# Squares and scaled norm tiles moved from SBUF to PSUM, and the first three projections after a norm run feature tile by feature tile

## The chip, the cores and the metric

The kernel runs on one core of a Trainium2 chip. The metric is the device time of one execution in microseconds. All arithmetic is float32; a product of two float32 matrices is made of three TensorE products of rounded parts (high times high, high times low, low times high).

Engines are named as the profile names them: PE is TensorE, PEld its weight loads, DVE is VectorE, ACT is ScalarE, POOL is GpSimd, SP is the engine that issues the DMAs. [...]

## The reference

Two layers of a transformer block with adaptive norms, on 512 tokens of width 1024, and a final norm. The four mixers are left out here, since the change does not touch them.

```python
def rmsnorm(x, g):
    y = xf * lax.rsqrt(jnp.mean(xf * xf, axis=-1, keepdims=True) + RMS_EPS)
    return (y * g).astype(x.dtype)

for l in range(DEPTH):                       # DEPTH = 2
    mod = c_act @ w_ada[l] + b_ada[l]
    sh1, sc1, g1, sh2, sc2, g2 = [t[:, None, :] for t in jnp.split(mod, N_ADA, axis=-1)]
    h = rmsnorm(x, norm_mix_g[l]) * (1.0 + sc1) + sh1
    z = h @ w_in[l]
    o = jnp.concatenate([swa_mixer(...), mla_mixer(...), nsa_mixer(...), moba_mixer(...)], axis=-1)
    x = x + g1 * (o @ w_out[l])
    h = rmsnorm(x, norm_mlp_g[l]) * (1.0 + sc2) + sh2
    x = x + g2 * (jnp.square(jax.nn.relu(h @ w_up[l])) @ w_down[l])
return rmsnorm(x, final_norm_g)
```

## The kernel before

The activations lie transposed: 8 feature tiles of 128 features (partitions) by 512 tokens (columns). The kernel is written with a scheduler that sets the order of each engine's queue when the program is built, from the program's own order, from what each instruction depends on and from an estimate of durations; the order is then fixed, and the scheduler adds the waits. Tiles come from pools with a fixed number of buffers for each tag; a new tile of a tag waits until the last reader of the tile that had its buffer is done.

PSUM has eight banks. Three belong to the tag `mm` (pool `psA`: the results of projections), two to `sc` (`psS`: attention scores and the broadcast of a norm), two to `pt` (`psT`: transposed attention weights), one to `po` (`psO`).

A product of a weight tile with the activations is `mm3` (lines 330 to 332): for each feature tile k three matmuls, high weight x high activation (L330), high weight x low activation (L331), low weight x high activation (L332). Weights come by DMA into a raw tile; ACT makes the high part (L89, `whi`), and POOL the low part by a subtraction of two tiles in SBUF (L91, `wlo`). There are four slots for high parts and four for low parts, and each is asked for three weight tiles ahead of its use. A slot falls free when the last matmul that reads it is done.

A norm and its neighbours run like this:

- `proj_x` (output projection, part 2, or down projection, part 5) makes the eight new tiles of the residual x. The first five are made over all 512 tokens. The last three (`HEAD = 3`) are made in two halves of 256 tokens: three groups for the first half, then `norm(0)`, then three groups for the second, then `norm(1)`. After each group DVE adds the result to x (L368), which also frees its PSUM bank.
- For each new tile of x, `Sums.add` squares it on ACT (L246, tile `sq`) and adds the square to a running sum on DVE (L247, `sqacc`); the very first square is written to the sum directly (L243).
- `norm_bcast` adds the sums over the partitions with four small matmuls (L277), raises to the power -1/2 on POOL (L257, after an L253 on DVE), and broadcasts the result to all partitions with matmuls (L263, tile `rsb`).
- `norm_tile` (L290 to L297) makes one feature tile of the normed activations for a half: DVE multiplies x by the gain column and `rsb` into a scaled tile t (L292, `ht`), ACT adds the shift and rounds to the high part (L294, `hhi`), DVE makes the low part from t, the shift and the high part (L295, `hlo`).
- `proj_head` (L336) makes the first three projections of the normed activations: all of the first half, group by group (for each group eight feature tiles), then all of the second half, group by group. Its three results take the three `mm` banks. Then the three evacuations follow, and `proj_T` makes the other projections one at a time, with 512 columns. In the MLP an evacuation is a relu on ACT (L1070), a square on DVE (L1071) and a split into high and low part (L398, L399). Before the mixers of layer 1 the first evacuation is a square and a scaled copy on ACT (L652, L653).

`tmp_tile` gives float32 tiles in SBUF, four buffers for all who use it, `sq` and `ht` among them. There are three places where norm and `proj_head` follow each other: in layer 0 before the MLP, in layer 1 before the mixers, and in layer 1 before the MLP. Layer 0 starts with `start` (L1085), which squares all of x, has a norm of its own (L1121 to L1131) while the weights of the adaptive part arrive and are reduced on DVE (L188), and runs the first five projections itself; of the lines changed it uses `Sums` alone. The final norm (`final_half`) uses `Sums` and writes its tiles out.

Of the kernel before, what the change touches and what calls it, by code (L numbers as in the profile page):

```python
# [10 lines left out]
F32 = mybir.dt.float32  # L11
F32R = mybir.dt.float32r
AF = mybir.ActivationFunctionType
ALU = mybir.AluOpType
# [3 lines left out]
P = 128  # L18
S = 512
D = 1024  # L20
KT = D // P
# [88 lines left out]
def layer_stack(ctx: ExitStack, tc: tile.TileContext, a, out):  # L110
    nc = tc.nc
# [8 lines left out]
    psT = ctx.enter_context(tc.tile_pool(name="psT", bufs=2, space=PSUM))  # L120
    psO = ctx.enter_context(tc.tile_pool(name="psO", bufs=1, space=PSUM))

    def mmbank(name):
        return psA.tile([P, 512], F32, tag="mm", name=name)

    def tmp_tile(name):
        return wkp.tile([P, S], F32, tag="tmp", name=name, bufs=4)
# [3 lines left out]
    X = {}  # L131
# [37 lines left out]
    for half in range(2):  # L169
        ps = psA.tile([P, 512], F32, tag="mm", name="cbp")  # L170
        for j in range(4):
            k = 4 * half + j
# [52 lines left out]
    H2 = S // 2  # L225

    def cols(half):
        return slice(0, S) if half is None else slice(half * H2, half * H2 + H2)

    class Sums:  # L230
# [6 lines left out]
        def add(self, k, half=None):  # L237
            for hv in (0, 1) if half is None else (half,):
                first = hv not in self.done
                self.done.add(hv)  # L240
            c = cols(half)
            if first:
                nc.scalar.activation(self.acc[:, c], X["x"][:, k, c], AF.Square)  # L243
            else:
                sq = tmp_tile("sq")
                nc.scalar.activation(sq[:, c], X["x"][:, k, c], AF.Square)  # L246
                nc.vector.tensor_tensor(self.acc[:, c], self.acc[:, c], sq[:, c], op=ALU.add)  # L247

# [39 lines left out]
        return gs  # L288

    def norm_tile(hh, k, c, rsb, gk, shk):  # L290
        t = tmp_tile("ht")
        nc.vector.scalar_tensor_tensor(t[:, c], X["x"][:, k, c], gk, rsb, op0=ALU.mult, op1=ALU.mult)  # L292
        hi, lo = hh[k]
        nc.scalar.activation(hi[:, c], t[:, c], AF.Identity, bias=shk)  # L294
        nc.vector.scalar_tensor_tensor(  # L295
            lo[:, c], t[:, c], shk, hi[:, c].bitcast(F32), op0=ALU.add, op1=ALU.subtract
        )  # L297

    def h_tiles(pool, tag, bufs):
# [5 lines left out]
    class Norm:  # L305
# [8 lines left out]
        def half(self, hv):  # L314
            rsb = norm_bcast(self.sums, hv)
            if self.hh is None:
                self.hh = self.mk()
                self.gcols = self.gs()
            for k in range(KT):
                norm_tile(  # L320
                    self.hh, k, cols(hv), rsb, self.gcols[:, k : k + 1],
                    mod[self.l][:, self.psh, k : k + 1],
                )


    def mm3(ps, w, h, k, first, last, c=slice(0, S)):

        wh, wl = w
        hh, hl = h
        nc.tensor.matmul(ps, wh[:, k, :], hh[:, c], start=first, stop=False)  # L330
        nc.tensor.matmul(ps, wh[:, k, :], hl[:, c], start=False, stop=False)  # L331
        nc.tensor.matmul(ps, wl[:, k, :], hh[:, c], start=False, stop=last)  # L332
# [3 lines left out]
    def proj_head(hs, evacs, step=None):  # L336

        evacs, rest = evacs[:HEAD], evacs[HEAD:]
        ws = [W.get() for _ in evacs]
        pss = [mmbank("pj") for _ in evacs]  # L340
        for half in range(2):
            c = cols(half)
            for g in range(len(evacs)):
                for k in range(KT):
                    mm3(pss[g][:, c], ws[g], hs[k], k, k == 0, k == KT - 1, c)
        for g, f in enumerate(evacs):
            f(pss[g])
            if step is not None:
                step()
        proj_T(hs, rest, step)  # L350

    def proj_T(hs, evacs, step=None):
        for f in evacs:
            w = W.get()
            ps = mmbank("pj")
            for k in range(KT):
                mm3(ps, w, hs[k], k, k == 0, k == KT - 1)
            f(ps)
            if step is not None:
                step()  # L360
# [41 lines left out]
    def attention_layer(l, n1, finish):  # L402
# [23 lines left out]
        with ExitStack() as es:  # L426
# [252 lines left out]
            if l == 0:  # L679
                for f, ps in zip(evacs[:3], pss):  # L680
                    f(ps)
            else:
                proj_head(hs, evacs[:3])
# [634 lines left out]
```

## Time and profile before

| | us |
|---|---|
| median of 3 runs | 1338.73 (1336.64 to 1339.17) |
| the profiled execution | 1340.61 |
| its span, first to last instruction | 1338.8 |
| PE busy in the span | 1257.1 (94%) |
| DVE, ACT, POOL busy | 765.2, 590.9, 512.1 |

A row of the timeline gives the start of an instruction (or of a run of equal ones, with x and their number), its duration, the engine, the line, what it writes and reads, and in brackets how long the engine had been idle before it and what ended that. The windows give for a stretch the busy time of PE with the number of its matmuls, the mean granted clock, and the traffic of the DMAs. Durations of matmuls overlap, so the distance between two starts is the better measure of their cost.

### The profile page before, as it was taken

The numbers are of one execution on the slowest core, as the hardware profiler recorded it, in microseconds if no ns is written. First come the engines' busy times: TensorE is split into PE (matmuls) and PEld (weight loads), VectorE is DVE, ScalarE is ACT, GpSimd is POOL, SyncE is SP. The second block draws the span as 40 slices with busy tenths as digits, with TensorE's granted clock in tenths as the row PEclk, the third lists the DMA queues.
The fourth block names the chain that finished last, engine by engine and source line by source line (L and its number), as shares of the span: only waits on it lengthen the run. The fifth ranks groups of instructions, "written<-read, shape, count | busy, mean of one in ns | idle before, by whom it ended". The sixth has DMA issues, their size and how long they took to land. (4 is left out here: it accounts for less than half of the span.)

```text
span 1338.8 us, 17560 instructions
## 1 busy us (share of the span) xinstructions
PE 1257.1 (94%) x6500; PEld 1049.3 (78%) x6500; DVE 765.2 (57%) x1609; ACT 590.9 (44%) x1145; POOL 512.1 (38%) x276
## 2 busy tenths in 40 slices
PE   3888999888999999999989899999999999999997
PEld 3676788768988888888889677878888888888886
DVE  6888878978445555454364887677753312213124
ACT  4346768683443132231234657687443313223220
POOL 4432232224344544545433432230534444444441
PEclk9989999999999999999989999999989999999999
DMA  8623233435246766766322221120423333333311
GB/s 334 209 98 127 64 111 111 140 126 206 69 131 185 244 212 209 239 190 204 130 93 90 94 95 64 51 74 11 166 80 94 94 95 95 96 97 98 102 49 64
DMA packets 49766, 168.69 MB, mean 126 GB/s; under 512 B 5648, under 2 KB 8336, under 8 KB 49680
## 3 DMA queue, kind: packets, MB, share of 16 engines
q1 hardware_dynamic: 49680, 167.57, 38.3%
q8 instruction: 51, 0.84, 0.2%
q14 instruction: 35, 0.29, 0.1%
HBM read 163.35 MB, written 4.19 MB: 125 GB/s over the span
## 5 line engine op out<-in xcount | busy, mean ns | idle before, releaser
L91 POOL TENSOR_TENSOR wlo<-raw,whi 128x1024 fp32r<-128x1024 f32 (+3 forms) x186 | 454.9, 2450 | 583.0 <-ACT whi L89 550.9
L89 ACT ACTIVATE whi<-raw 128x1024 fp32r<-128x1024 f32 (+3 forms) x186 | 193.7, 1045 | 437.7 <-PE px L331 237.5
L331 PE MATMUL pj<-hlo,whi 128*128 128x512 f32 (+1 forms) x783 | 297.3, 380 | 8.5 <-DVE hlo L295 8.4
L330 PE MATMUL pj<-hhi,whi 128*128 128x512 f32 (+1 forms) x783 | 296.0, 380 | 2.6 <-ACT hhi L1124 1.2
L332 PE MATMUL pj<-hhi,wlo 128*128 128x512 f32 (+1 forms) x783 | 294.7, 376 | 0.0
L330 PE MATMUL px<-a,whi 128*128 128x512 f32 (+1 forms) x560 | 208.4, 372 | 0.0
L332 PE MATMUL px<-a,wlo 128*128 128x512 f32 (+1 forms) x560 | 208.1, 372 | 0.0
L331 PE MATMUL px<-a,whi 128*128 128x512 f32 (+1 forms) x560 | 207.4, 370 | 0.0
L331 PEld LDWEIGHTS pj<-hlo,whi 128*128 128x128 f32 x783 | 150.8, 193 | 35.5 <-DVE hlo L295 11.4
L330 PEld LDWEIGHTS pj<-hhi,whi 128*128 128x128 f32 x783 | 150.4, 193 | 28.0 <-ACT hhi L1124 2.2
L332 PEld LDWEIGHTS pj<-hhi,wlo 128*128 128x128 f32 x783 | 150.7, 192 | 25.8
L368 DVE SCALAR_TENSOR_TENSOR x<-px,mod,x 128x512 f32<-128x512 f32 (+1 forms) x92 | 62.1, 678 | 171.1 <-PE px L332 162.1
L1071 DVE SCALAR_TENSOR_TENSOR t<-pj,r 128x512 f32<-128x512 f32 x64 | 44.3, 692 | 157.8 <-ACT r L1070 157.8
L188 DVE CUSTOM_DVE_ANT_0 adaw<-adaw,cb,vecs 128x1024 f32<-128x1024 f32 x78 | 105.2, 1349 | 43.8 <-DMA adaw<-in_wadaD 43.7
L332 PEld LDWEIGHTS px<-a,wlo 128*128 128x128 f32 x560 | 105.1, 188 | 19.2
L331 PEld LDWEIGHTS px<-a,whi 128*128 128x128 f32 x560 | 105.1, 188 | 18.8
L330 PEld LDWEIGHTS px<-a,whi 128*128 128x128 f32 x560 | 105.2, 188 | 17.9
L399 DVE TENSOR_TENSOR a<-t,a 128x512 fp32r<-128x512 f32 x64 | 71.8, 1122 | 44.7 <-ACT a L398 44.7
L540 ACT ACTIVATE e<-e,nm 128x256 f32<-128x256 f32 (+3 forms) x160 | 85.9, 539 | 14.6 <-DVE nm L535 14.4
L518 POOL TENSOR_SCALAR e<-e,rc 128x128 f32<-128x128 f32 x40 | 24.3, 608 | 143.2 <-DVE rc L545 67.1
L399 DVE TENSOR_TENSOR pl<-pt,ph 128x512 fp32r<-128x512 f32 (+1 forms) x112 | 65.3, 597 | 4.4 <-ACT ph L398 3.3
L574 PE MATMUL pt<-ident,e 128*128 128x128 f32 x376 | 61.7, 278 | 3.6 <-DVE pl L399 1.5
(236 smaller groups left out, 1932.7 us busy)
## 6 DMA issues: line engine op xcount, KB each, us to landing
adaw<-in_wadaD SPq DMA_DIRECT2D x78, 512.0 KB, 4.4
raw<-in_wup SPq DMA_DIRECT2D x64, 512.0 KB, 3.5
raw<-in_wdown SPq DMA_DIRECT2D x64, 512.0 KB, 3.5
raw<-in_winT SPq DMA_DIRECT2D x28, 512.0 KB, 3.6
ada<-in_wadaP SPq DMA_DIRECT2D x16, 512.0 KB, 7.2
raw<-in_wout SPq DMA_DIRECT2D x16, 512.0 KB, 3.5
x<-in_xT SPq DMA_DIRECT2D x8, 512.0 KB, 5.1
cw<-in_cw SPq DMA_DIRECT2D x8, 512.0 KB, 4.9
```

The lines of the kernel that those rows point to most:

```text
L89: self.nc.scalar.activation(vh[0:rows], raw[0:rows], AF.Copy)
L91: eng.tensor_tensor(vl[0:rows], raw[0:rows], vh[0:rows].bitcast(F32), op=ALU.subtract)
L188: nc.vector.tensor_tensor_reduce(out=w, in0=w, in1=cb, scale=1.0, scalar=vecs[:, off : off + 1], op0=ALU.mult, op1=ALU.add, accum_out=mod[ ...
L330: nc.tensor.matmul(ps, wh[:, k, :], hh[:, c], start=first, stop=False)
L331: nc.tensor.matmul(ps, wh[:, k, :], hl[:, c], start=False, stop=False)
L332: nc.tensor.matmul(ps, wl[:, k, :], hh[:, c], start=False, stop=last)
L368: last["dve"] = nc.vector.scalar_tensor_tensor(X["x"][:, m, c], ps, mod[l][:, part, m : m + 1], X["x"][:, m, c], op0=ALU.mult, op1=ALU.add)
L399: last["dve"] = nc.vector.tensor_tensor(lo, src, hi.bitcast(F32), op=ALU.subtract)
L518: nc.gpsimd.tensor_scalar_mul(e, e, r)
L540: nc.scalar.activation(e, e, AF.Exp, bias=nm[:, n : n + 1], scale=-1.0, accum_out=den[:, n : n + 1])
L574: nc.tensor.transpose(pt[:, c : c + P], p[n][:, col : col + P], ident)
L1071: nc.vector.scalar_tensor_tensor(t, ps, 0.0, r, op0=ALU.max, op1=ALU.mult)
```

## The change

Three edits. The square of `Sums.add` and the scaled tile of `norm_tile` are taken from the tag `pt` in PSUM (two buffers, shared with each other and with the transposes of attention) instead of from the four SBUF buffers of `tmp_tile`; the scaled tile takes a whole bank and uses 256 of its columns. And in `proj_head` the loops over feature tiles and over the three groups change places: in each half, the three matmuls of group 0, 1 and 2 for feature tile 0, then for feature tile 1, and so on.

```diff
@@ Sums.add
-                sq = tmp_tile("sq")
+                sq = psT.tile([P, S], F32, tag="pt", name="sq")
                 nc.scalar.activation(sq[:, c], X["x"][:, k, c], AF.Square)
                 nc.vector.tensor_tensor(self.acc[:, c], self.acc[:, c], sq[:, c], op=ALU.add)
@@ norm_tile
-        t = tmp_tile("ht")
-        nc.vector.scalar_tensor_tensor(t[:, c], X["x"][:, k, c], gk, rsb, op0=ALU.mult, op1=ALU.mult)
+        t = psT.tile([P, 512], F32, tag="pt", name="ht")[:, 0:H2]
+        nc.vector.scalar_tensor_tensor(t, X["x"][:, k, c], gk, rsb, op0=ALU.mult, op1=ALU.mult)
         hi, lo = hh[k]
-        nc.scalar.activation(hi[:, c], t[:, c], AF.Identity, bias=shk)
+        nc.scalar.activation(hi[:, c], t, AF.Identity, bias=shk)
         nc.vector.scalar_tensor_tensor(
-            lo[:, c], t[:, c], shk, hi[:, c].bitcast(F32), op0=ALU.add, op1=ALU.subtract
+            lo[:, c], t, shk, hi[:, c].bitcast(F32), op0=ALU.add, op1=ALU.subtract
         )
@@ proj_head
-            for g in range(len(evacs)):
-                for k in range(KT):
+            for k in range(KT):
+                for g in range(len(evacs)):
                     mm3(pss[g][:, c], ws[g], hs[k], k, k == 0, k == KT - 1, c)
```

## Rows read from the trace of the kernel before

**Rows 1.** The page, part 1: busy us (share of the span), number of instructions.

```profile
PE 1257.1 (94%) x6500; PEld 1049.3 (78%) x6500; DVE 765.2 (57%) x1609; ACT 590.9 (44%) x1145; POOL 512.1 (38%) x276
```

**Rows 2.** Four lines of DVE: ns shortest/median/longest, first and last start, shapes.

```profile
L295 DVE SCALAR_TENSOR_TENSOR hlo<-ht,mod,hhi x48: 468/478/2500, 321.4 to 983.8; 128x256 fp32r<-128x256 f32 x48
L247 DVE TENSOR_TENSOR sqacc<-sqacc,sq x47: 409/679/2927, 6.7 to 1329.5; 128x256 f32<-128x256 f32 x24, 128x512 f32<-128x512 f32 x23
L368 DVE SCALAR_TENSOR_TENSOR x<-px,mod,x x92: 469/750/752, 297.1 to 1328.4; 128x512 f32<-128x512 f32 x68, 128x256 f32<-128x256 f32 x24
L399 DVE TENSOR_TENSOR pl<-pt,ph x112: 403/678/693, 111.0 to 930.7; 128x512 fp32r<-128x512 f32 x72, 128x256 fp32r<-128x256 f32 x32, 128x384 fp32r<-128x384 f32 x8
```

**Rows 3.** Groups by line, DVE, 682 to 697 us: busy us, mean ns, idle before.

```profile
L295 DVE SCALAR_TENSOR_TENSOR hlo<-ht,mod,hhi 128x256 fp32r<-128x256 f32 x8 | 9.3, 1166 | 0.3 <-ACT hhi L294 0.3
```

**Rows 4.** Timeline of DVE and of POOL, layer 1 before the mixers.

```profile
684.72 2.34 DVE L295 SCALAR_TENSOR_TENSOR hlo<-ht,mod,hhi 128x256 fp32r<-128x256 f32 x1
...
684.37 2.41 POOL L91 TENSOR_TENSOR wlo<-raw,whi 128x1024 fp32r<-128x1024 f32 x1 [2.86 <-ACT whi L89]
687.03 2.41 POOL L91 TENSOR_TENSOR wlo<-raw,whi 128x1024 fp32r<-128x1024 f32 x1 [0.26 <-ACT whi L89]
```

**Rows 5.** Timeline of PE, same place.

```profile
695.85 0.58 PE L331 MATMUL pj<-hlo,whi 128*128 128x256 f32 x1 [1.93 <-DVE hlo L295]
```

**Rows 6.** Windows: length, PE busy (matmuls), granted clock, DMA share and GB/s.

```profile
327.00:351.80 24.80, 22.27 (x154) 0.86 0.16 52
688.60:696.00 7.40, 3.87 (x22) 0.95 0.53 185
696.00:702.00 6.00, 5.96 (x27) 0.50 0.30 90
702.00:715.00 13.00, 13.00 (x111) 1.00 0.34 110
...
965.80:991.40 25.60, 22.13 (x154) 0.87 0.20 62
```

**Rows 7.** Timeline of PE, layer 0, output projection and norm before the MLP.

```profile
297.95 0.47 PE L330 MATMUL px<-ohi,whi 128*128 128x512 f32 x1 [2.65 <-DVE x L368]
...
317.19 0.61 PE L277 MATMUL rsb<-ones,sqacc 128*128 128x1 f32 x4 [1.23 <-DVE sqacc L247]
...
318.85 0.71 PE L263 MATMUL rsb<-ident,rs 128*128 128x128 f32 x4 [0.48 <-POOL rs L257]
```

**Rows 8.** Timeline of DVE and ACT, second half of the norm at 700 us.

```profile
700.50 1.26 DVE L292 SCALAR_TENSOR_TENSOR ht<-x,gs,rsb 128x256 f32<-128x256 f32 x3 [2.09 <-PE rsb L263]
701.69 1.27 DVE L295 SCALAR_TENSOR_TENSOR hlo<-ht,mod,hhi 128x256 fp32r<-128x256 f32 x3
...
701.02 1.31 ACT L294 ACTIVATE hhi<-ht,mod 128x256 fp32r<-128x256 f32 x3 [6.52 <-DVE ht L292]
```

**Rows 9.** Windows of PE around 300 and 320 us, columns as in rows 6.

```profile
299.50:302.80 3.30, 3.30 (x9) 0.51 1.03 402
319.70:323.20 3.50, 3.50 (x19) 0.51 0.02 6
```

**Rows 10.** Timeline of ACT and DVE, evacuations in layer 1, MLP and mixers.

```profile
985.92 1.06 ACT L89 ACTIVATE whi<-raw 128x1024 fp32r<-128x1024 f32 x1 [2.18 <-issue]
987.01 0.60 ACT L1070 ACTIVATE r<-pj 128x512 f32<-128x512 f32 x1
...
988.90 1.04 ACT L89 ACTIVATE whi<-raw 128x1024 fp32r<-128x1024 f32 x1
...
987.64 0.69 DVE L1071 SCALAR_TENSOR_TENSOR t<-pj,r 128x512 f32<-128x512 f32 x1 [3.38 <-ACT r L1070]
...
710.49 0.68 ACT L653 ACTIVATE ckvg<-pj,vecs 128x512 f32<-128x512 f32 x1
```

**Rows 11.** Timeline of DVE and PE, start of layer 0.

```profile
9.88 5.03 DVE L247 TENSOR_TENSOR sqacc<-sqacc,sq 128x512 f32<-128x512 f32 x4
...
59.55 0.97 PE L330 MATMUL pj<-hhi,whi 128*128 128x512 f32 x3 [1.23 <-ACT hhi L1124]
```

## Prediction

> **What bounds the kernel now.** Read the page's busy times first. PE is busy 1257.1 of 1338.8 us [rows 1], so a change is worth what it takes out of PE's 82 us of idle time, or out of stretches where PE runs at a low clock. Nothing else reaches the end. The change touches the norms, so I looked at the three places where a half of a norm is followed by the first three projections: A (layer 0, before the MLP, 327 to 352 us), B (layer 1, before the mixers, 689 to 715) and C (layer 1, before the MLP, 966 to 991).
>
> Then the single lines, with their shortest, median and longest duration. L295, which makes the low part of a tile, takes 468 to 2500 ns in one shape, and L247 up to 2927; L368, of the same operation as L295 but with one input in PSUM, never takes over 752 in 92 (512 columns the most of them), nor L399 with its source in PSUM over 693 [rows 2]. L295 and L247 read two tiles in SBUF. In the first half at B eight L295 take 9.3 us [rows 3] where 8 x 0.478 would be 3.8, and the timeline shows what stretches three of them: one runs from 684.72 for 2.34 us, exactly while POOL runs an L91 (684.37 for 2.41 us) [rows 4]. A and C have the same pattern, three L295 of sixteen.
>
> [...]
>
> **Part 1: scaled tile and squares in PSUM.** L295 and L247 then have one input in PSUM and one in SBUF, as L368 and L399 have, so I price them at the shortest of those, 469 and 403 ns, and take all stretching away [rows 2]. Writing a tile to PSUM from DVE or ACT is not in the trace. The nearest rows are the same operations into SBUF and the PSUM reads of rows 2. I take no difference, with 60 ns either way per instruction: 22 tile and square operations a half, 1.3 us of DVE work beside PE work. [...]
>
> What is this worth? The floor of a place is 144 matmuls of 128x256 (2 halves x 3 groups x 8 tiles x 3). At full clock 111 take 13.0 us [rows 6], 0.117 each, so 16.9 us. With the four sums (0.61) and four broadcasts (0.71) of the second half [rows 7] it is 18.2 us. The stretches from the first matmul of the head to the end of its last are 24.8 us (A), 26.4 (B: 7.4, 6.0 and 13.0) and 25.6 (C) [rows 6]. Excess over the floor: 6.6, 8.2 and 7.4 us.
>
> All of it comes from late tiles, and it goes: DVE has 16 norm operations, 3 updates and 3 sums to do for a half, 22 x 0.4 us (the spacing of L292 and L295 where nothing holds them, 1.27 for three [rows 8]) = 9 us, while PE has 8.5 us of output projection or down projection (72 matmuls) between the broadcast and the head, and then 8.5 us of head. What remains is the chain from the sums to the broadcast through POOL, for which PE waits 0.48 us at full clock [rows 7]: 0.5 us a place.
>
> At A, DVE is late once more before the first broadcast: PE waits 1.23 us for L247 [rows 7] behind a stretched one, and 3.5 us at 0.51 follow [rows 9], 1.7 lost. I take the 1.2 and half of the 1.7: 2.1.
>
> **Part 2: two buffers instead of four.** A new tile waits until the tile two before it has been read by ACT and DVE; what queues behind it is DVE's next low part and update. One round trip is 0.52 us from L292 to L294, 0.67 to L295 and 0.4 for that [rows 8], about 1.6 us; two slots give a tile every 0.8 us, which is what DVE needs for its two operations anyway. Cost nothing in the first half (hidden by the 72 matmuls) and nothing in the second, if both slots serve tiles.
>
> **Part 3: tile by tile.** PE now takes nine matmuls per tile, 1.06 us, instead of three, 0.35, so it no longer overtakes tiles that come every 0.8 us. In the first half part 1 has made that needless; in the second it covers up to (0.8 - 0.35) x 7 = 3 us, already in the floor above. It has two costs.
> At the start all three banks and all three weights are wanted within 0.7 us instead of over 5.6. The third weight's low part is ready at 687.03 + 2.41 = 689.44 at B [rows 4], wanted at 688.6 + 8 x 0.117 = 689.5; the third bank is free one L368 (0.48) after the last px matmul. I take 0.3 us a place (0 to 1).
> At the end all three groups stop within 0.7 us, and the fourth projection needs a bank of the same three. Before, the first group ended 5.6 us earlier and its evacuation was hidden. Now PE stands, with everything behind it, until L1070 and L1071 have read the first bank. ACT has L89 in front: at C an L89 (1.06) goes ahead of L1070 (0.60), then L1071 (0.69) [rows 10]. Two weight slots fall free together, and both casts were asked for earlier than the evacuations, so I expect two L89 first: the first starts 0.85 us before the last matmul ends, so 2 x 1.0 - 0.85 + 0.6 + 0.7 + 0.1 = 2.5 us of idle PE at A and C. At B the evacuation is two ACT operations (L653, the second, takes 0.68 [rows 10]) behind the casts of narrower weight tiles: 2.0. Bounds: 1.7 with one L89 ahead, 3.6 with three.
> After 2.65 us of idle PE at 297.95 [rows 7] the clock was 0.51 for 3.3 us [rows 9], a loss of 1.6. I charge that at A and C, and half at B.
>
> **Part 4: the start.** Four L247 take 5.03 us [rows 11] instead of 4 x 0.68 [rows 2]: 2.3 less, but with two slots each square waits for the sum two before it, which gives back 0.6. Of the 1.7 us, how much reaches PE? PE's last wait there is 1.23 us for a tile at 59.55 [rows 11]. I take 1.2 (0 to 2.3). The last norm has no stretched operation in its chain: 0.
>
> **The sum.** A: 6.6 - 0.5 - 0.3 - 2.5 - 1.6 = 1.7. B: 8.2 - 0.5 - 0.3 - 2.0 - 0.8 = 4.6. C: 7.4 - 0.5 - 0.3 - 2.5 - 1.6 = 2.5. Together 8.8, with 2.1 before A and 1.2 at the start 12.1 us. The profiled execution took 1340.61 us (span 1338.8), 1.9 above the median of the runs; 12.1 off the median of 1338.73 is 1326.6.
>
> **Rivals.**
> *Cheap end.* One L89 goes ahead (1.7 us, 1.2 at B) and the clock holds. Then A gives 4.1, B 6.2, C 4.9, the stretch before A 2.9, the start 1.7: 19.8 us, 1319. For it: at C the second L89 (988.90) came after the first L1070 (987.01) [rows 10], if only because its slot fell free later.
> *Dear end.* Three casts ahead (3.6 us; 3.1 at B) and, as at B now, 6 us at half clock (3.0) [rows 6]: A -0.8, B 1.3, C 0, the rest 1.7: about 2 us, 1336.5. For it: PE has nothing else to run there.
> *Starved norm, slower.* The squares share the two slots. If one slot is held by a square or by the order of the queues while tiles are made, a tile takes the whole 1.6 us; eight take 12.8, and in the second half PE, which starts 3 us after the broadcast and needs 1.06 us a tile, waits 3.1 us and loses 1.6 to 3 of clock. It decides from a tile spacing of 1.06 us on. At 5.4 us in three places, 16 off the gain: 1342. Against it: the second half's squares are summed before its tiles. [...]
> *No relief.* L295 stays stretched with one PSUM input. Part 3 then hides the first half's waits, the second half's sums stay late, and the end costs the same: 0 to 3 us, 1337. Against it: none of the 92 L368 is [rows 2].
>
> **How the numbers follow.** Forecast 0.51, cheap end 0.19, dear end 0.14, starved 0.11, no relief 0.05. A measurement here can tell about 0.2% (2.7 us) from no change. Faster: forecast and cheap end, 0.70. Within: dear end and part of no relief, 0.17. Slower: starved and the tail of the dear end, 0.13. The forecast alone spans 1321 to 1333; to hold 8 in 10 the range goes from 1316 (all of A's and the start's bounds favourable) to 1338.
>
> **What would show it.** Right: no L295 or L247 over 0.8 us; PE without idle between the last px matmul and the end of the head, but idle of 2 to 2.5 us ahead of the fourth projection, with two L89 ahead of the first evacuation on ACT. Wrong: L295 still at 2.3 us beside L91; tiles of a half over 1.06 us apart; or PE idle inside the second half. The weakest numbers are the order on ACT at the end of the head and the clock after it.

## The result: 1.2 to 1.5% faster

The changed kernel takes 1321.63 us, the median of four runs (1317.07 to 1323.52), beside 1337.68 for the kernel before (1335.35 to 1339.17): a ratio of 0.988 (95% interval 0.985 to 0.990), 16 us. Repeated on another occasion it took 1317.08 (median of five, 1314.81 to 1324.56) beside 1337.72, a ratio of 0.985 (0.983 to 0.988). The forecast was 1326.6 with a range of 1316 to 1338. In the changed kernel every line from 291 on has a number higher by one: L292 is now L293, L295 is L296, L330 is L331, L1070 is L1071.

The profiled execution took 1317.07 us (span 1315.3), 23.5 us less than that of before. That is more than the medians differ by, since the one profile is the shortest of its four runs and the other longer than the runs beside it. First the busy times (page, part 1, to be set beside [rows 1]), and then four lines with shortest, median and longest duration (beside [rows 2]):

```profile
PE 1244.1 (95%) x6500; PEld 1039.2 (79%) x6500; DVE 725.4 (55%) x1609; ACT 588.3 (45%) x1145; POOL 512.9 (39%) x276
```

```profile
L296 DVE SCALAR_TENSOR_TENSOR hlo<-ht,mod,hhi x48: 473/480/485, 310.7 to 958.8; 128x256 fp32r<-128x256 f32 x48
L247 DVE TENSOR_TENSOR sqacc<-sqacc,sq x47: 410/424/689, 7.0 to 1305.4; 128x256 f32<-128x256 f32 x24, 128x512 f32<-128x512 f32 x23
L246 ACT ACTIVATE sq<-x x47: 387/390/604, 6.4 to 1305.0; 128x256 f32<-128x256 f32 x24, 128x512 f32<-128x512 f32 x23
L295 ACT ACTIVATE hhi<-ht,mod x48: 455/474/477, 310.2 to 958.3; 128x256 fp32r<-128x256 f32 x48
```

POOL does what it did, and DVE is 40 us less busy: no L296 takes over 485 ns, no L247 over 689. That is not because they no longer meet POOL's L91. Before, 9 L295 and 15 L247 started while an L91 ran, and every one of them took over 0.75 us; now 21 L296 and 18 L247 start so, and none does. Then PE: at A all idle times of over 0.2 us from the last output projections on, and at all three places the first matmul of the fourth projection (beside [rows 5] and [rows 7]).

```profile
308.15 0.71 PE L263 MATMUL rsb<-ident,rs 128*128 128x128 f32 x4 [0.48 <-POOL rs L257]
320.91 0.61 PE L277 MATMUL rsb<-ones,sqacc 128*128 128x1 f32 x4 [0.26 <-DVE sqacc L247]
322.55 0.71 PE L263 MATMUL rsb<-ident,rs 128*128 128x128 f32 x4 [0.45 <-POOL rs L257]
336.51 0.50 PE L331 MATMUL pj<-hhi,whi 128*128 128x512 f32 x1 [2.53 <-DVE t L1072]
...
696.01 0.50 PE L331 MATMUL pj<-hhi,whi 128*128 128x512 f32 x1 [2.00 <-ACT ckvg L654]
...
966.18 0.50 PE L331 MATMUL pj<-hhi,whi 128*128 128x512 f32 x1 [2.53 <-DVE t L1072]
```

A "head" is from here on what `proj_head` runs on PE at one of the three places, both halves. Inside the heads hardly anything is left but the chain through POOL (0.44 to 0.52 us, at B and C too); ahead of the fourth projection stands a new wait of 2.53, 2.00 and 2.53 us. The windows (columns after PE: PEld, DVE, ACT, POOL busy, granted clock, DMA share, GB/s; beside [rows 6]) show the head with its wait, and the 6.8 us behind it, at A, B and C:

```profile
314.60:336.51 21.91, 18.67 (x156) 18.06 (x154) 12.30 (x31) 10.56 (x21) 6.13 (x4) 1.00 0.20 62
336.51:343.30 6.79, 6.79 (x23) 5.42 (x24) 5.76 (x5) 2.81 (x5) 5.37 (x3) 0.75 0.58 168
674.70:696.01 21.31, 18.79 (x155) 18.36 (x154) 10.75 (x27) 9.64 (x20) 6.04 (x5) 1.00 0.40 131
696.01:702.80 6.79, 6.79 (x42) 6.07 (x43) 2.94 (x6) 2.58 (x5) 3.87 (x4) 1.00 0.42 118
944.60:966.18 21.58, 18.61 (x155) 18.09 (x153) 11.45 (x29) 10.16 (x20) 6.16 (x4) 1.00 0.21 68
966.18:973.00 6.82, 6.82 (x29) 5.58 (x30) 5.79 (x5) 3.92 (x7) 5.41 (x3) 1.00 0.54 161
```

The granted clock, a share that in the traces of before and after is 0.50 or 1.00 at every moment, fell behind the wait at A (0.75 over these 6.8 us: 0.57 up to 339.9 us, 0.93 from there on) and stayed at 1.00 at B and C. What stands in front of the first evacuation is on ACT, at A:

```profile
333.24 2.00 ACT L89 ACTIVATE whi<-raw 128x1024 fp32r<-128x1024 f32 x2 [3.10 <-PE pj L332]
335.15 1.06 ACT L1071 ACTIVATE r<-pj 128x512 f32<-128x512 f32 x2
```

And at C the chain that ended last (start, duration) runs through just this:

```profile
963.88 1.04 ACT whi L89
964.92 0.49 ACT r L1071
965.44 0.70 DVE t L1072
966.18 0.50 PE pj L331
```

The same PE matmuls, paired one to one in both traces, say where the 23.5 us were won. The last output projections before A start 9.2 us earlier; 3.1 more are won up to the first matmul of the head at A; A itself brings 1.3 (with what follows it), B 7.0, C 2.7, and 0.2 is won in each of the halves ahead of B, of C and at the end. (That is 24.0 at the last matmul; 0.5 is lost again behind it.)

### The profile page after: what moved, and what is told of

It reads as the page before. It is cut to its first block, busy times and chain, and to the rows that moved or that the text cites. A ratio compares the mean times of both kernels' runs of the same rounds, so it can differ in the third digit from the quotient of the medians.

```text
span 1315.3 us, 17552 instructions
## 1 busy us (share of the span) xinstructions
PE 1244.1 (95%) x6500; PEld 1039.2 (79%) x6500; DVE 725.4 (55%) x1609; ACT 588.3 (45%) x1145; POOL 512.9 (39%) x276
## 5 line engine op out<-in xcount | busy, mean ns | idle before, releaser
L91 POOL TENSOR_TENSOR wlo<-raw,whi 128x1024 fp32r<-128x1024 f32 (+3 forms) x186 | 455.9, 2456 | 570.8 <-ACT whi L89 539.6
L89 ACT ACTIVATE whi<-raw 128x1024 fp32r<-128x1024 f32 (+3 forms) x186 | 193.5, 1045 | 444.4 <-PE px L332 247.0
L331 PE MATMUL pj<-hhi,whi 128*128 128x512 f32 (+1 forms) x783 | 294.0, 377 | 8.5 <-DVE t L1072 5.1
L332 PE MATMUL pj<-hlo,whi 128*128 128x512 f32 (+1 forms) x783 | 292.5, 374 | 0.0
L331 PE MATMUL px<-a,whi 128*128 128x512 f32 (+1 forms) x560 | 208.6, 372 | 0.0
L331 PEld LDWEIGHTS pj<-hhi,whi 128*128 128x128 f32 x783 | 148.0, 189 | 33.9 <-DVE t L1072 5.5
L332 PEld LDWEIGHTS pj<-hlo,whi 128*128 128x128 f32 x783 | 148.0, 189 | 25.3 <-DVE hlo L1130 0.3
L333 PEld LDWEIGHTS pj<-hhi,wlo 128*128 128x128 f32 x783 | 147.6, 189 | 25.7
L188 DVE CUSTOM_DVE_ANT_0 adaw<-adaw,cb,vecs 128x1024 f32<-128x1024 f32 x78 | 105.7, 1355 | 45.6 <-DMA adaw<-in_wadaD 45.5
L332 PEld LDWEIGHTS px<-a,whi 128*128 128x128 f32 x560 | 105.1, 188 | 18.9
L331 PEld LDWEIGHTS px<-a,whi 128*128 128x128 f32 x560 | 105.2, 188 | 17.9
L400 DVE TENSOR_TENSOR a<-t,a 128x512 fp32r<-128x512 f32 x64 | 74.7, 1169 | 41.8 <-ACT a L399 41.8
```

Source lines behind the costliest of these rows:

```text
L89: self.nc.scalar.activation(vh[0:rows], raw[0:rows], AF.Copy)
L91: eng.tensor_tensor(vl[0:rows], raw[0:rows], vh[0:rows].bitcast(F32), op=ALU.subtract)
L188: nc.vector.tensor_tensor_reduce(out=w, in0=w, in1=cb, scale=1.0, scalar=vecs[:, off : off + 1], op0=ALU.mult, op1=ALU.add, accum_out=mod[ ...
L400: last["dve"] = nc.vector.tensor_tensor(lo, src, hi.bitcast(F32), op=ALU.subtract)
```

## The experiments

All ran beside the kernel before, whose median was 1337.72, 1337.12 and 1336.96 us on three occasions (1335.82 in one run beside the last experiment). Ratios are given with their 95% intervals. A head is counted from the start of its first matmul to the start of its 144th, from the starts in the trace; the stall is PE's idle time ahead of the fourth projection; "early" is how much sooner than in the profile of before the last output projections ahead of A start (290.05 us there).

| kernel | median us | ratio | head A, B, C | stall A, B, C | early |
|---|---|---|---|---|---|
| before | 1337 to 1338 | | 24.7, 26.2, 25.5 | 0, 0, 0 | |
| the change | 1321.63 | 0.988 (0.985 to 0.990) | 19.0, 18.9, 18.7 | 2.53, 2.00, 2.53 | 9.2 |
| the change again | 1317.08 | 0.985 (0.983 to 0.988) | 19.0, 19.0, 18.7 | 2.53, 2.00, 2.53 | 7.7 |
| PSUM, old order | 1313.18 | 0.981 (0.980 to 0.983) | 19.1, 19.0, 18.7 | 0.64, 0, 0 | 6.0 |
| new order alone | 1350.61 | 1.009 (1.007 to 1.011) | 23.5, 25.9, 25.5 | 2.67, 2.00, 2.67 | -0.1 |
| two orders | 1311.31 | 0.980 (0.979 to 0.981) | 19.1, 18.9, 18.7 | 0.65, 0, 0 | 7.0 |
| squares of the start alone | 1331.56 | 0.997 (0.996 to 0.999) | 23.8, 26.0, 25.6 | 0, 0, 0 | 8.5 |
| squares alone | 1332.15 | 0.996 (0.994 to 0.997) | 23.8, 25.8, 25.5 | 0, 0, 0 | 7.6 |
| tile alone | 1326.68 | 0.993 (0.990 to 0.995) | 19.5, 23.3, 21.4 | 0, 0, 0 | 1.1 |
| the change, casts late | 1316.15 | 0.984 (0.982 to 0.986) | 19.0, 18.9, 18.7 | 1.58, 1.24, 1.58 | 9.2 |
| the change, one slot | 1330.60 | 0.995 (0.994 to 0.997) | 21.7, 20.9, 20.8 | 2.79, 2.25, 2.77 | 10.1 |
| tile and new order | 1336.05 | 0.999 (0.998 to 1.001) | 19.0, 21.7, 20.0 | 2.56, 2.00, 2.53 | 1.3 |
| two orders, casts late | 1309.06 | 0.979 (0.977 to 0.982) | 19.1, 18.9, 18.7 | 0, 0, 0 | 4.6 |
| before, POOL with one input | 1308.07, one run | | 19.3, 19.7, 19.3 | 0, 0, 0 | 9.9 |

The experiments are written on the kernel before and have its line numbers, unless said otherwise.

**PSUM, old order.** The first two edits of the change without the third.

```diff
 in proj_head, as before:
             for g in range(len(evacs)):
                 for k in range(KT):
```

> Scaled tile and squares in PSUM, the loop of the first three projections group by group as before. Theory (late tiles were the excess, and the new loop order pays a stall of 2.5, 2.0 and 2.5 us at the end of the three heads): no idle time of over 0.5 us ahead of the fourth projection, no half clock behind it; the first half's tiles come 0.9 us apart where PE wants one every 0.35, so 1.5 to 1.9 us of waits in each first half and up to 0.5 in the second. From the kernel before: 3.8 at A, 5.8 at B, 5.0 at C, as much ahead of A and at the start as the change has; so 0 to 4 us faster than the change. Rival (the loop order is what removes the waits of the first half, and the casts on ACT make tiles late in PSUM too): waits of 3 us and more in each first half, with half clock behind them, 3 to 8 us slower than the change.

It is 24.5 us faster than before, and 4 to 8 faster than the change. The waits that I expected in the first halves are not there: the heads are as short as the change's. The tiles come no sooner (at A the last low part of the first half is done at 322.47 us, and the first group alone would have wanted it at 320.8), yet PE does not wait, so matmuls of other groups must stand in between. The rows name no group; that the scheduler put them there because it reckoned a tile late is my reading. The loop order in the program is only a wish. The third edit is thus not needed, and it costs the stalls that it was charged with, all but the 0.64 us that are left at A without it.

**New order alone.** Tile and squares in SBUF as before, and only the loops exchanged.

```diff
-            for g in range(len(evacs)):
-                for k in range(KT):
+            for k in range(KT):
+                for g in range(len(evacs)):
```

> Only the loop order changed, tile and squares in SBUF as before. Theory: L295 and L247 are stretched to over 2 us as before; the first half's waits vanish, since a tile is then wanted every 1.06 us, but the second half's sums are as late as before (wait of 1.3 to 2 us for the sums, about 2 us for the first tile), and the end of the head stalls 2.0 to 2.5 us. Within 2.5 us of the kernel before, on either side. Rival (the loop order carries the gain): 8 us and more faster than the kernel before.

Both were wrong: it is 13 us slower. The stalls at the end are there (7.3 us in all), but the heads are hardly shorter than before: what the order saves inside them, a new wait at their start takes back. Beside them the profile shows a lower clock behind the stalls at A and B (0.69 over the next 5.4 us and 0.81 over the next 8.8) and a head that starts 1 us later at A. The wait at the start, in the timeline of PE, DVE and POOL at B, in this order:

```profile
696.66 0.55 PE L330 MATMUL pj<-hhi,whi 128*128 128x256 f32 x1 [3.09 <-ACT sq L246]
...
691.43 0.47 DVE L368 SCALAR_TENSOR_TENSOR x<-px,mod,x 128x256 f32<-128x256 f32 x1
691.82 2.33 DVE L295 SCALAR_TENSOR_TENSOR hlo<-ht,mod,hhi 128x256 fp32r<-128x256 f32 x1
...
696.04 0.47 DVE L368 SCALAR_TENSOR_TENSOR x<-px,mod,x 128x256 f32<-128x256 f32 x1
...
691.48 2.39 POOL L91 TENSOR_TENSOR wlo<-raw,whi 128x1024 fp32r<-128x1024 f32 x1 [0.26 <-ACT whi L89]
```

After three matmuls PE wants the second group's bank. An update (L368) frees it, and that update stands on DVE behind an L295 of 2.33 us that POOL's L91 stretches. It ends at 696.51 and PE goes on 0.15 us later; the profile names an L246 that ended just then too.

**Tile and new order.** To try that reading: the third edit with the scaled tile in PSUM and the squares in SBUF.

```diff
+        t = psT.tile([P, 512], F32, tag="pt", name="ht")[:, 0:H2]
 ... (norm_tile as in the change; in proj_head:)
+            for k in range(KT):
+                for g in range(len(evacs)):
```

> The change without its squares: the scaled tile in PSUM, the new loop order, all squares in SBUF. It tells what made the loop order alone 13 us slower. Theory (a bank that PE wants early is freed by an update queued behind a stretched L295): with L295 short the 3 us wait at the start of the heads is gone; what stays is the end (2.5, 2.0 and 2.5 us) and late sums; 0 to 6 us slower than the tile alone in the old order (1326.7), 1327 to 1333. Rival (the loop order itself costs 4 us a place): 1336 to 1342.

The waits for a bank at the start of the heads shrink from 3.28, 3.09 and 3.05 us (at A in two parts) to 1.34, 0.96 and 0.86, so the stretched L295 was some two thirds of them; here the profile names the update (PE at 689.58, "0.96 <-DVE x L368"). But in time the rival is right: 9.4 us slower than the tile in the old order, some 3 us a place. It is not the start of the heads that costs this. In spite of the waits there they are 0.5, 1.5 and 1.5 us shorter than with the tile alone. What costs is their end: the stalls (2.56, 2.00 and 2.53 us) and a lower clock behind all three, 0.55, 0.75 and 0.60 over the next 3.4 us, where with the tile alone it was 1.00.

**Two orders.** Tile and squares in PSUM, the first half tile by tile, the second group by group.

```diff
+            for k, g in ([(k, g) for k in range(KT) for g in range(3)] if half == 0
+                         else [(k, g) for g in range(3) for k in range(KT)]):
```

> Tile and squares in PSUM, first half tile by tile, second half group by group. Theory: the first half hides late tiles as the change does, the second half lets the first group end 5.6 us before the third, so that its evacuation is hidden: no wait over 0.5 us ahead of the fourth projection, at most 1 us of waits for tiles in a second half. 7 us saved at the three ends and up to 2 of clock, less 1.5 to 3 for the tiles: 3 to 7 us faster than the change, about 1315 to 1319 us. Rival (casts ahead of the evacuations on ACT delay the fourth projection whatever the order): the same 2 to 2.5 us of idle time ahead of it, the change's time.

The theory holds. At A two L89 still stand ahead of the first evacuation, but the first group is done so early that 0.65 us are left of the stall:

```profile
337.15 0.50 PE L330 MATMUL pj<-hhi,whi 128*128 128x512 f32 x1 [0.65 <-DVE t L1071]
...
333.88 2.01 ACT L89 ACTIVATE whi<-raw 128x1024 fp32r<-128x1024 f32 x2 [1.33 <-PE pj L331]
335.80 1.06 ACT L1070 ACTIVATE r<-pj 128x512 f32<-128x512 f32 x2
```

6 to 10 us faster than the change, and the same on ACT and DVE, instruction for instruction, as PSUM with the old order. Those two differ by 1.9 us, and their intervals overlap; the orders of the first half can't explain a difference, since the heads are equal.

**The change again.** 

> The changed kernel once more, beside the others. Its first profile was 23.5 us shorter than that of the kernel before, 9.2 of them gained before the first output projection of layer 0, where its medians differ by 16 us. If the early gain belongs to the change, the same stretch is again 8 to 10 us earlier in this profile; if those two executions differed by chance, it is 1 to 5 us. Time 1317 to 1324.

7.7 us early: a little under the 8 to 10, and well above the 1 to 5 of chance, so most of the early gain is the change's own. A, B and C bring 1.4, 6.9 and 4.1.

**Squares of the start alone.**

```diff
 Sums.add, in start alone:
-                sq = tmp_tile("sq")
+                sq = psT.tile([P, S], F32, tag="pt", name="sq")
```

> Only the squares of the first norm, at the start of layer 0, in PSUM; everything else as before. The order fixed for the engines then differs from the kernel before in three places of the first 25 us alone: on DVE the second tile's L188 goes ahead of the first L1121 instead of behind it, on POOL one L91 ahead of L257, on ACT one L89 ahead of the last square. Theory (the whole early gain comes from there): first projection 2.8 us earlier, first output projection of layer 0 6 to 9 us earlier, layer 1 unchanged behind that; 1328 to 1332 us. Rival (the prediction's size): 1 to 2.3 us, 1335.5 to 1337.

8.5 us early, as much as the change, and all three heads close to those of before (A is 0.9 us shorter): the early gain is the start's. In time the interval is 1.2 to 5.9 us: less than the profile shows, and upward from the prediction's 1.2. Timeline of DVE and PE in this run:

```profile
18.34 1.28 DVE L188 CUSTOM_DVE_ANT_0 ada<-ada,cb,vecs 128x1024 f32<-128x1024 f32 x1
...
21.27 0.75 DVE L1121 SCALAR_TENSOR_TENSOR ht<-x,gs,rsb 128x512 f32<-128x512 f32 x1 [1.64 <-PE rsb L263]
...
22.82 1.65 PE L1146 MATMUL pj<-hhi,whi 128*128 128x512 f32 x3 [1.59 <-ACT hhi L1124]
...
81.17 0.39 PE L734 MATMUL mv<-whi,ckh 128*128 128x256 f32 x1 [0.68 <-ACT gates L691]
```

The broadcast is no earlier than before (L1121 starts at 21.27, before at 21.32), because POOL now does two L91 ahead of its L257. But the second L188 has gone ahead of the first L1121, into time in which DVE had stood idle for 2.84 us. The next tile and PE's first projection come 2.8 us earlier; at 81 us a wait for ACT's gates (L691) is 0.68 instead of 2.60 us, which makes 4.8. Another 2.0 us are a matter of which engine was first. Here is one instruction of layer 0's mixers, which no edit touches, in the kernel before and then in this run:

```profile
251.51 2.57 DVE L520 TENSOR_SCALAR e<-e,rc 128x512 f32<-128x512 f32 x1
...
245.49 0.47 DVE L520 TENSOR_SCALAR e<-e,rc 128x512 f32<-128x512 f32 x1
```

Before, an L91 had started 0.07 us ahead of it (251.44, for 2.35 us); it was stretched like the others, though it reads only one full tile, and PE then waited 2.04 us at 254.46. Here it started 0.18 us ahead of the L91 (245.67), and PE has no such wait. Of the nine executions with all squares of the start in PSUM, three have the wait (PSUM in the old order and both versions with two orders), and they are the least early ones, 4.6 to 7.0 us; the other six are 7.6 to 10.1. So some 2 us of the early gain are luck. The remaining 1.7 us I have not followed.

**Squares alone.**

```diff
-                sq = tmp_tile("sq")
+                sq = psT.tile([P, S], F32, tag="pt", name="sq")
```

> All squares in PSUM, the scaled tile in SBUF, loop order as before. Theory: the start's 6 to 9 us, and up to 3 ahead of A, where the sum that the broadcast waits for is no longer stretched; L295 is still stretched to over 2 us and the three heads stay 23 to 26 us long. 1326 to 1331 us. Rival (the sums are what makes the second halves late): heads 2 to 4 us shorter, 1318 to 1324.

The theory's mechanism, with heads of 23.8, 25.8 and 25.5 us, and a time 1 us above its range. The two lines of DVE:

```profile
L247 DVE TENSOR_TENSOR sqacc<-sqacc,sq x47: 403/423/690, 6.8 to 1316.7; 128x256 f32<-128x256 f32 x24, 128x512 f32<-128x512 f32 x23
L295 DVE SCALAR_TENSOR_TENSOR hlo<-ht,mod,hhi x48: 469/477/2337, 312.5 to 971.6; 128x256 fp32r<-128x256 f32 x48
```

**Tile alone.**

```diff
-        t = tmp_tile("ht")
+        t = psT.tile([P, 512], F32, tag="pt", name="ht")[:, 0:H2]
 ... (the rest of norm_tile as in the change)
```

> The scaled tile in PSUM, all squares in SBUF, loop order as before. Theory: no L295 over 0.5 us, heads of 19 to 20 us with no stall of over 1 us behind them, 5.5 to 7 us each, 17 to 20 us in all; no gain at the start and little ahead of A, since L247 is still stretched. 1318 to 1322 us. With the squares' part it must come to what both together gave with this loop order (1313.2, 24.5 us). Rival (L247 takes over as the late one): heads of 21 us and more, 1324 to 1330.

```profile
L247 DVE TENSOR_TENSOR sqacc<-sqacc,sq x47: 411/693/2707, 6.8 to 1317.9; 128x256 f32<-128x256 f32 x24, 128x512 f32<-128x512 f32 x23
L295 DVE SCALAR_TENSOR_TENSOR hlo<-ht,mod,hhi x48: 466/477/485, 321.5 to 972.4; 128x256 fp32r<-128x256 f32 x48
```

Each edit frees just its own line. Here the rival is right: L247 takes over as the late one, and the heads at B and C stay at 23.3 and 21.4 us. So the two edits are not a sum: 5.0 and 10.4 us alone, 24.5 together.

**The change, casts late.** Only one weight is cast ahead while the head fetches its three.

```diff
+        ahead, W.split_ahead = W.split_ahead, 1
         ws = [W.get() for _ in evacs]
         pss = [mmbank("pj") for _ in evacs]
+        W.split_ahead = ahead
```

> The changed kernel with one edit: while the head's three weights are fetched, only one further weight is cast ahead, so that one L89 instead of two stands on ACT ahead of the first evacuation; the next one comes behind the first evacuations. Theory (the stall at the end of the head is two casts, then evacuation): idle time ahead of the fourth projection 1.0 us shorter at A and C, 1.5 to 1.6 instead of 2.5, at B 1.1 to 1.3 instead of 2.0; 2 to 4 us faster than the change, 1314 to 1319. Rival (the bank itself, or the fourth weight's low part, is what is late): still 2.5 us, the change's time.

```profile
333.17 1.06 ACT L89 ACTIVATE whi<-raw 128x1024 fp32r<-128x1024 f32 x1 [3.10 <-PE pj L331]
334.13 1.07 ACT L1070 ACTIVATE r<-pj 128x512 f32<-128x512 f32 x2
335.09 1.06 ACT L89 ACTIVATE whi<-raw 128x1024 fp32r<-128x1024 f32 x1
```

One cast less in front, and the stall is shorter by one cast: 0.95, 0.76 and 0.95 us. The stall is made of casts, then evacuation. In time, 1 to 5.5 us below the two measurements of the change, it can't be told from the nearer one.

**Two orders, casts late.** Both edits together.

> The version with two orders (first half tile by tile, second half group by group, 1311.3 us) and only one further weight cast ahead while the head's weights are fetched. Theory: the 0.65 us that was left ahead of the fourth projection at A goes too, the rest is as it was: 1309 to 1312 us. Rival (the casts that come later are late for the fifth and sixth projections): idle time of over 1 us there, 1313 to 1317.

The last 0.65 us at A is gone. 1309.06 is the lowest time of a kernel that computes everything, but its interval overlaps that of the two orders alone.

**The change, one slot.** The scaled tile in the one buffer of another bank.

```diff
-        t = psT.tile([P, 512], F32, tag="pt", name="ht")[:, 0:H2]
+        t = psO.tile([P, 512], F32, tag="po", name="ht")[:, 0:H2]
```

> The changed kernel with one buffer for the scaled tile instead of two (another bank of PSUM), the squares in the two buffers of before. The prediction's starved norm, made on purpose: each tile waits until ACT and DVE have read the one before it. Prediction's price: 1.6 us a tile, 3.1 us of waits and up to 3 of clock in each second half, 16 us in three places; 12 to 18 us slower than the change, 1331 to 1337. Rival (the order fills the time and the tiles come about 1.1 us apart, as fast as PE takes them): at most 4 us slower, 1318 to 1323.

DVE in the second half at A, first here, then in the change:

```profile
322.55 0.49 DVE L292 SCALAR_TENSOR_TENSOR ht<-x,gs,rsb 128x256 f32<-128x256 f32 x1
323.58 0.48 DVE L295 SCALAR_TENSOR_TENSOR hlo<-ht,mod,hhi 128x256 fp32r<-128x256 f32 x1 [0.54 <-ACT hhi L294]
324.10 0.49 DVE L292 SCALAR_TENSOR_TENSOR ht<-x,gs,rsb 128x256 f32<-128x256 f32 x1
```

```profile
323.30 0.88 DVE L293 SCALAR_TENSOR_TENSOR ht<-x,gs,rsb 128x256 f32<-128x256 f32 x2 [1.58 <-PE rsb L263]
324.33 0.88 DVE L296 SCALAR_TENSOR_TENSOR hlo<-ht,mod,hhi 128x256 fp32r<-128x256 f32 x2 [0.15 <-ACT hhi L295]
325.12 0.87 DVE L293 SCALAR_TENSOR_TENSOR ht<-x,gs,rsb 128x256 f32<-128x256 f32 x2
```

One buffer gives a tile every 1.55 us (322.55 to 324.10), two give two every 1.82. The heads are 1.9 to 2.7 us longer, which is the prediction's mechanism, and the time is 9 to 13.5 us above the change's. But of the 15.5 us between the two profiles the heads make only 6.7, and their clock is 1.00 throughout: the 1.6 to 3 us of clock that the prediction charged inside them is not there. Another 7 us were lost behind the head of B, where after a wait of 2.25 us PE ran at a granted clock of 0.50 for 8 us (windows of this run); the change, after 2.00 us, ran on at 1.00.

```profile
701.75:705.20 3.45, 3.45 (x9) 2.87 (x10) 0.75 (x1) 2.59 (x5) 1.95 (x2) 0.50 0.51 137
705.20:710.00 4.80, 4.80 (x24) 4.70 (x23) 0.00 (x0) 0.00 (x0) 0.00 (x0) 0.50 0.29 106
```

**Before, POOL with one input.** In the kernel before, POOL's subtraction (two inputs) is replaced by a product with zero (one input); the low parts of the weights are then zero, so their share of the products is left out. Lines behind 92 have a number higher by one; the new operation is L93.

```diff
 where POOL makes the low part:
-            eng.tensor_tensor(vl[0:rows], raw[0:rows], vh[0:rows].bitcast(F32), op=ALU.subtract)
+            eng.tensor_scalar(vl[0:rows], vh[0:rows].bitcast(F32), 0.0, 0.0, op0=ALU.mult, op1=ALU.add)
```

> The kernel before, with one edit on POOL's side: the low part of the weights is no longer raw minus high part (two inputs) but the high part times zero (one input, so the low parts are zero and their share of the products is left out); same tiles, same place in the order, same matmuls. Theory (a VectorE operation with both inputs in SBUF stands still until the POOL operation that runs has ended, whatever POOL's operation is): L295 and L247 are still stretched, up to the duration of the new POOL operation plus 0.1 to 0.3 us. Rival (only POOL's two-input operation gets in the way): no L295 over 0.55 us, heads of 19 to 20 us.

The line of L296 (L295 before), then POOL and DVE at B:

```profile
L296 DVE SCALAR_TENSOR_TENSOR hlo<-ht,mod,hhi x48: 469/478/987, 311.4 to 951.2; 128x256 fp32r<-128x256 f32 x48
```

```profile
667.50 1.06 POOL L93 TENSOR_SCALAR wlo<-whi 128x1024 fp32r<-128x1024 f32 x1 [2.87 <-ACT whi L89]
...
667.85 0.99 DVE L296 SCALAR_TENSOR_TENSOR hlo<-ht,mod,hhi 128x256 fp32r<-128x256 f32 x1
```

The new operation takes 1.06 us where L91 took 2.41, and an L296 that starts inside it ends 0.28 us after it (668.84 and 668.56), as the L295 of before ended 0.28 after the L91 [rows 4]. So here POOL's operation stretched it although it reads one tile only, and by as much less as it was itself shorter (0.99 us where that L295 took 2.34). With 1.06 instead of 2.41 us the heads are 19.3 to 19.7 us long with all tiles in SBUF, without a stall behind them; the time, below the change's, is of one run, and POOL is shorter everywhere in it.

Together the rows show this: in the kernel before, all nine L295 that started while an L91 ran ended 0.28 to 0.29 us after it, here those two that were stretched at B 0.27 and 0.28 us after the L93, and with one input in PSUM, in the change, no L296 took over 485 ns and no L247 over 689, though 21 and 18 of them started while an L91 ran.

## Why the prediction was right, and where it was not

**Part 1 held, for both lines separately.** 9 of 48 L295 and 15 of 47 L247 took over 0.75 us before, none after. PE stood idle for L295 12 times before, 8.4 us in all, and for L296 not once. The excess of the heads over the floor of 18.2 us was to fall to 0.5 + 0.3; the heads are 19.0, 18.9 and 18.7 us. The wait through POOL is 0.44 to 0.52 us, and the 2.1 us ahead of A are 3.1. PSUM cost next to nothing here: L296 480 ns where L295 took 478, L293 482 where L292 took 474; on ACT L246 takes 390 instead of 420 (medians over both shapes) and L295 474 where L294 took 495. That is 2 and 8 ns more on DVE and 20 to 30 less on ACT.

The 60 ns either way that the prediction allows for an instruction were an estimate of mine, and no run shows them: not in L296, and not in L247, whose shortest takes 410 ns beside 409 before.

**Part 2 held in kind.** Two buffers give a tile every 0.91 us, not 0.8, still under the 1.06 from which it decides; and the squares didn't starve the tiles. The run with one slot shows what lay beyond, and that the rival's wait of 3.1 us was too high: by the prediction's own numbers eight tiles are done after 12.8 us, and PE would begin the last after 3 + 7 x 1.06 = 10.4, a wait of 2.4; the heads became 1.9 to 2.7 us longer.

**Part 3, the end of the head, held.** 2.5, 2.0 and 2.5 us were predicted, 2.53, 2.00 and 2.53 measured, with two L89 in front of the first evacuation, and the run with late casts takes away one cast's worth. (Its 1.58 us are what the prediction's sum gives with one cast, 1.0 - 0.85 + 0.6 + 0.7 + 0.1 = 1.55; the bound of 1.7 that it states was not that sum.) The wait at the start, 0.3, didn't show; a bank and a weight were ready in time, but only because the updates on DVE were: in the run of the new order alone that same step costs 3.1 us at B and C.

**The clock was the mis-sized term.** I charged 1.6 us at A and C and 0.8 at B. At A it is 1.7 (the gain, 18.0 us at the head's last matmul, is 15.3 at the first matmul behind the wait and 13.6 some fifteen matmuls later). At B and C it is nothing, in both profiles of the change, though C stood idle for the same 2.53 us as A. So of 4.0 us 2.3 were not paid; that B and C kept the clock is luck as far as the runs show, since in others they lost it behind waits of the same length (see the end). At B a stretch at a clock of 0.54 in the kernel before, behind the head, went as well, which no step had (windows of before):

```profile
718.90:722.30 3.40, 3.40 (x10) 2.60 (x10) 3.12 (x7) 0.16 (x1) 1.64 (x1) 0.54 0.31 122
```

With that B brought 7.0 instead of 4.6. At C, 2.7 stands close to the 2.5 by chance: 4.2 were won up to the fourth projection (25.64 to 21.47 us from the head's start), and then the 312 matmuls to the end of the up projection took 72.67 us instead of 71.18; in the second profile of the change they took 71.31, and C brought 4.1.

**The start was the step that failed.** "Of the 1.7 us, how much reaches PE? I take 1.2 (0 to 2.3)" priced shorter operations in an order that was taken as given. But other buffers change what the scheduler holds to be ready, and it set the order anew: an L188 went into DVE's idle time ahead of the first tile. (Whether it is the place of the buffers or their number that makes the scheduler do so, no run separates.) PE's first projection alone starts 2.8 us earlier, and nine executions with the squares in PSUM are 4.6 to 10.1 us early, three with them in SBUF, and POOL as before, -0.1 to 1.3. In the profiles this is most of what the forecast of 1326.6 lacked, though some 2 us of it hang on which of two engines comes first at 250 us. In time, where the start alone brings 1.2 to 5.9 us, how much of the 5 to 9.5 us it explains is open.

**The rivals.** The times came out near the cheap end (1319), but not by its mechanism: two casts, not one, went ahead, and of its two conditions only the clock came true, at B and C. The starved norm is real with one buffer and not with two. No relief and the dear end did not occur.

**What the prediction didn't ask** is whether the third edit is needed. Its own text had it: "In the first half part 1 has made that needless". With tile and squares in PSUM the old order is as short inside the heads and has no stall of over 0.64 us behind them; the new order gives 4 to 8 us back there, and with tiles in SBUF it costs 13.

## What to carry to other kernels

Where an operation of one shape takes five times its shortest duration, look at what the engine next to it runs during just those microseconds: here moving one of two inputs to PSUM took the whole stretch away (the longest 485 ns instead of 2500), and shortening the neighbour's operation from 2.41 to 1.06 us shortened it (to 987 ns). If several lines suffer from the same neighbour, treat all of them, since the one left over takes the place of the other. And an order that makes several results end together should be used only where nothing waits for the first of them.

## What the runs showed of the hardware that I had not expected

A lower granted clock did not follow every wait of the same length: after 2.53 us of idle PE it was 0.52 to 0.55 for the next 3.4 us at A and 1.00 at C, in the same kernel, in both of its profiles. Nor is it the place: with the tile and the new order alone it was 0.60 at C behind the same 2.53 us, and 0.75 at B behind the 2.00 us after which the change kept 1.00. What decides it no run here shows. Here is the second profile of the change, the wait and the 3.4 us behind it at A, then at C (windows):

```profile
335.50:338.05 2.55, 0.03 (x1) 0.00 (x0) 0.74 (x2) 2.55 (x5) 2.12 (x1) 0.99 0.00 0
338.05:341.50 3.45, 3.45 (x8) 2.77 (x9) 2.68 (x3) 2.18 (x4) 3.45 (x3) 0.52 0.48 152
965.00:967.58 2.58, 0.06 (x1) 0.00 (x0) 0.74 (x2) 2.58 (x5) 2.13 (x1) 1.00 0.00 0
967.58:971.00 3.42, 3.42 (x15) 2.83 (x16) 2.65 (x3) 2.19 (x4) 3.42 (x3) 1.00 0.53 153
```

And at a granted clock of 1.00 the matmuls of 512 columns started 0.227 to 0.230 us apart on average in every long stretch of four profiles but one, 976 to 1036 us of the first profile of the change, where it was 0.2333; what slowed them by 2% there is open.
